# A two-layer backbone with a product-key mixer: layer 1's modulation moved into layer 0's one-hot blocks, and the advance steps regrouped

## The chip, the cores and the metric

The kernel runs on one core of a Trainium2 chip. The metric is the time of one execution on the device in microseconds (us), the median over runs. The names of the engines are those of the profile: PE is TensorE (matmuls), PEld its weight loads, DVE is VectorE, ACT is ScalarE, POOL is GpSimd, SP is the queue from which nearly all transfers are issued.

## The reference

256 latent tokens and 256 context tokens, width 1024, go through two layers. Every layer first turns the conditioning vectors into six rows of modulation, normalizes and modulates, mixes the tokens (attention and retention in layer 0, differential attention in layer 1), and then sends each token to 128 of 16384 experts:

```
mod = jax.nn.silu(c) @ ada_w[l] + ada_b[l]          # (1024,) @ (1024, 6144), and the same for c_ctx
sh1, sc1, g1, sh2, sc2, g2 = jnp.split(mod, 6)
x = x + g1 * mixer(modulate(rmsnorm(x), sh1, sc1))
h2 = modulate(rmsnorm(x), sh2, sc2)
# _peer, for each block of 128 tokens
s = einsum('thpd,hpnd->thpn', (h2 @ w_q).reshape(128, 8, 2, 128), keys)
s_top, i_top = lax.top_k(s, 16)                     # for each of 8 heads and 2 halves
cand = s_top[:, :, 0, :, None] + s_top[:, :, 1, None, :]
best, pos = lax.top_k(cand, 16)                     # 16 of 256 sums; eid is the pair of indices
gate = softmax(best)
act = gelu(einsum('td,thkd->thk', h2, u_tab[eid]))
f = einsum('thk,thkd->td', gate * act, v_tab[eid])
x = x + g2 * f
```

## The kernel before

Everything is fp32, the large products as sums of split parts (high and low) on PE. The stages follow one another: the even mixer (layer 0), layer 0's routing, its one-hot blocks, its main loop over 128 groups of 128 experts, then the odd mixer (layer 1) and the same three stages of the mixer of experts for layer 1.

**Modulation.** `mod_group` computes one of six groups of a layer's modulation in eight k-slices. A slice is one load of 512 KB of `ada_w` (tile `w`, by `wload`) and eight small matmuls into `mod_ps` (four column quarters, two parts each). After the eighth slice the rows go through `mrow` and two matmuls into `mcol`. Before the change, four groups of layer 0 and two of layer 1 are spread as fill over the even mixer; the other four groups of layer 1 are spread over the odd mixer, where DVE makes the products (`macc`) and PE only sums over the partitions at the end of a group.

**Routing.** `peer_route` makes the queries and scores head by head on PE, copies them (ACT, `S`), and `top16` on DVE takes the 16 best of each half. `route_heads` is called twice for each stream of 256 tokens (two streams in layer 0, one in layer 1), with r=0 in the middle and with r=1 behind the last scores: candidate sums `cand`, a second `top16`, and the indices by one-hot comparisons (`ab`, `abf`, `rk`, `oh`). The results, transposed (`trp`), are the slots `sl` of the blocks.

**u steps.** `First` runs ahead of the main loop: `ahead` yields one step for each group of 128 experts, 27 of them in layer 0 and 22 in layer 1. A step loads `ur` (512 KB), splits it into `uh` (ACT) and `ul` (GpSimd or DVE), and makes 24 matmuls into `u_ps`; ACT then takes the gelu. Steps are issued during `route_heads` with r=1, then between the blocks, then behind them.

**One-hot blocks.** 24 in layer 0, 12 in layer 1. `find` and `weigh` are four large operations of DVE, `join` is 32 matmuls into `g_ps` and `keep` copies to `stage` (ACT) and writes 1 MB to `gd`. `pipeline` issues the blocks in a staggered way, so that different blocks stand in different stages. Afterwards `G` is read back from `gd`, and the first product `y` of the main loop needs it.

What order the work has is decided by the order in which the code issues it: each engine and the SP queue take their instructions in order.

Of the kernel before, what the change touches and what calls it, by code (L numbers as in the profile page):

```python
# [19 lines left out]
D = 1024  # L20
# [10 lines left out]
FILL0, FILL1 = (1, 2, 2, 1), (0, 2, 2, 2)  # L31
NUS = (2, 3)
NRAW, NWQ = 3, 6
# [5 lines left out]
ROUTE, AFTER = (12, 9), (3, 4)  # L39
# [3 lines left out]
def backbone(ctx: ExitStack, tc: tile.TileContext, x, cx, ccT, ada_w, ada_b, ada_rows, n1g, n2g, ev_in, ev_out,  # L43
# [114 lines left out]
    def wload(src, kn, nn):  # L158
        w = P["wp"].tile([128, kn, nn], F32, tag="w", name="w", bufs=NW)
        last["w"] = nc.sync.dma_start(w, src.rearrange("(k p) n -> p k n", p=128))  # L160
        return w
# [42 lines left out]
    def mod_group(d, l, g, both=True):  # L204

# [8 lines left out]
        if both:  # L214
            p = mm([128, 256], "mod_ps")
        else:
            acc = P["z"].tile([128, D], F32, tag="macc", name="macc", bufs=1)
        for k in range(KD):
            w = wload(ada_w[l, k * 128:(k + 1) * 128, g * D:(g + 1) * D], 1, D)
            if both:  # L220
                matmuls(silu_c[:, k, :], w[:, 0], k == 0, k == KD - 1)
            elif k == 0:
                nc.vector.tensor_scalar(acc, w[:, 0], silu_c[:, 0, 0:1], None, op0=OP.mult)
            else:
                nc.vector.scalar_tensor_tensor(acc, w[:, 0], silu_c[:, k, 0:1], acc, op0=OP.mult, op1=OP.add)
            yield
        if not both:
            p = mm([128, 256], "mod_ps")
            matmuls(ones[:, 0:32], acc, True, True)
# [376 lines left out]
    def odd_mixer(mod, fill):  # L606
# [27 lines left out]
        with in_order():  # L634
            norm_T((0,), aff1, hi, lo, t2)
            project(hi, lo, od_in, 0, 512, 512, tiles[:2], to_tiles(qq, 512), fill, FILL1[0])
        norm_T((1,), aff1, hi, lo, t2)
        project(hi, lo, od_in, 512, 1024, 512, tiles[:2], to_tiles({tk: qq[tk][:, 512:] for tk in qq}, 512), fill, FILL1[0])
        for tk in (0, 1):
            heads_T(qT, tk, qq[tk])  # L640
        project(hi, lo, od_in, 1024, 2048, 512, tiles, to_tiles(kk, 512), fill, FILL1[1])
# [4 lines left out]
        def values_of(n):  # L646
            project(hi, lo, od_in, 2048 + n * 512, 2560 + n * 512, 512, tiles, to_tiles({tk: vv[tk][:, n * 512:] for tk in vv}, 512), fill, FILL1[2 + n])
            if n:
                for _ in fill:
                    pass  # L650
# [73 lines left out]
    def route_heads(r, m, ix, ixb, i12, gate, step):  # L724
# [5 lines left out]
        for a in range(2):  # L730
            nc.scalar.copy(ixb[:, a].rearrange("p n (i h) -> p i h n", i=2), ix[:, :, hs, a, :])
        cand = wk([128, 2, 4, 112], "cand")
        for i in range(2):
            nc.gpsimd.tensor_tensor(cand[:, i, :, 0:64].rearrange("p h (a b) -> p h a b", a=4),
                                    m[:, i, hs, 0, 0:4, None].to_broadcast([128, 4, 4, 16]),
                                    m[:, i, hs, 1, None, :].to_broadcast([128, 4, 4, 16]), op=OP.add)
            nc.gpsimd.tensor_tensor(cand[:, i, :, 64:112].rearrange("p h (a b) -> p h a b", a=12),
# [4 lines left out]
        for i in range(2):  # L742
            for h in range(4):
                top16(best[:, i, h, :], pos[:, i, h, :], cand[:, i, h, :])
                if h % 2:
                    step()
        pi = pos.rearrange("p i h k -> p k (i h)").bitcast(I32)
# [6 lines left out]
        nc.scalar.copy(abf, ab.rearrange("p a f k n -> p a f (k n)"))  # L754
# [7 lines left out]
        nc.vector.tensor_add(rf, rf, abf[:, :, 0, :])  # L762
        for a in range(2):
# [9 lines left out]
            step()  # L773
        g = wk([128, 8, 16], "gate_e")
        b3 = best.rearrange("p i h k -> p (i h) k")
        nc.vector.tensor_sub(g, b3, b3[:, :, 0:1].to_broadcast([128, 8, 16]))
        nc.scalar.activation(g, g, AF.Exp)
        gs = sm([128, 8], "gs")
        nc.vector.tensor_reduce(gs, g, axis=AX.X, op=OP.add)
        nc.vector.reciprocal(gs, gs)  # L780
        nc.gpsimd.tensor_mul(gate[:, :, r * 64:(r + 1) * 64].rearrange("p i (h k) -> p i h k", h=4), g.rearrange("p (i h) k -> p i h k", i=2),
# [489 lines left out]
```

## Time and profile before

| | us |
|---|---|
| median of 3 runs | 2745.76 (2743.51 to 2748.35) |
| the profiled execution, its own time | 2754.86 |
| its span, first to last instruction | 2752.8 |
| PE busy | 2570.1 (93%) |
| DVE busy | 2055.0 (75%) |
| ACT busy | 1120.4 (41%) |
| POOL busy | 1043.0 (38%) |

Rough borders of the stages in the profiled execution: even mixer to 333 us, layer 0's routing to 546, its blocks and the rest of the u steps to 717, its main loop to 1690, odd mixer to 1930, layer 1's routing to 2054, its blocks and u steps to 2150, its main loop to 2740. A row of a timeline gives the start, the duration, the engine, the line of the kernel, the operation with output and inputs, and in brackets how long the engine stood idle before it and whose end released it.

### The profile page before, as it was taken

The numbers are of one execution on the slowest core, as the hardware profiler recorded it, in microseconds if no ns is written. First come the engines' busy times: TensorE is split into PE (matmuls) and PEld (weight loads), VectorE is DVE, ScalarE is ACT, GpSimd is POOL, SyncE is SP. The second block draws the span as 40 slices with busy tenths as digits, with TensorE's granted clock in tenths as the row PEclk, the third lists the DMA queues.
The fourth block names the chain that finished last, engine by engine and source line by source line (L and its number), as shares of the span: only waits on it lengthen the run. The fifth ranks groups of instructions, "written<-read, shape, count | busy, mean of one in ns | idle before, by whom it ended". The sixth has DMA issues, their size and how long they took to land.

```text
span 2752.8 us, 39475 instructions
## 1 busy us (share of the span) xinstructions
PE 2570.1 (93%) x14787; PEld 2237.7 (81%) x14787; DVE 2055.0 (75%) x3753; ACT 1120.4 (41%) x1832; POOL 1043.0 (38%) x643
## 2 busy tenths in 40 slices
PE   7899996899999999999999998989859999999997
PEld 4776775899989888899898876756859899999995
DVE  3535579898677776677677776787888788888888
ACT  3234432444333333333333334234535455555543
POOL 0201042300477677667766610100520344434431
PEclk9999997899999999999999998999979999999999
DMA  8562431255888888888888875632537999999996
GB/s 285 178 207 96 138 99 33 85 207 221 293 288 287 288 287 297 286 294 298 296 308 279 289 251 165 226 129 89 179 108 257 341 347 345 348 349 332 355 326 217
DMA packets 263552, 667.80 MB, mean 243 GB/s; under 512 B 21760, under 2 KB 108544, under 8 KB 258752
## 3 DMA queue, kind: packets, MB, share of 16 engines
q1 hardware_dynamic: 204176, 458.81, 48.9%
q0 software_dynamic: 55296, 201.35, 20.2%
q10 hardware_dynamic: 3888, 5.11, 0.6%
q8 instruction: 116, 1.90, 0.3%
q14 instruction: 76, 0.62, 0.1%
HBM read 621.88 MB, written 42.47 MB: 241 GB/s over the span
## 4 chain that ended last, share of the span: by engine, by line
PE 70%; DVE 13%; issue 5%; POOL 5%; DMA 4%; ACT 1%; ACTq 0%; POOLq 0%; SPq 0%; DVEq 0%
PE y L1038 24%; PE u_ps L911 9%; PE u_ps L910 9%; PE u_ps L909 9%; PE g_ps L985 4%; PE z_ps L318 2%; PE z_ps L319 2%; PE z_ps L320 2%; POOL ul L155 2%; POOL row L859 2%; DMA w<-in_ada_w_dram 1%; PE trp L170 1%; PE q_ps L806 1%; PE q_ps L807 1%; PE q_ps L805 1%
## 5 line engine op out<-in xcount | busy, mean ns | idle before, releaser
L909 PE MATMUL u_ps<-hi,uh 128*128 128x384 f32 (+1 forms) x2048 | 635.7, 310 | 42.8 <-ACT uh L154 35.6
L1038 PE MATMUL y<-vh,ww 128*128 128x512 f32 x2304 | 661.4, 397 | 7.0 <-ACT ww L1019 6.1
L911 PE MATMUL u_ps<-hi,ul 128*128 128x384 f32 (+1 forms) x2048 | 637.5, 311 | 24.8 <-POOL ul L155 13.9
L910 PE MATMUL u_ps<-lo,uh 128*128 128x384 f32 (+1 forms) x2048 | 634.6, 310 | 0.0
L1038 PEld LDWEIGHTS y<-vh,ww 128*128 128x128 f32 x2304 | 425.0, 189 | 95.0 <-ACT ww L1019 11.4
L859 POOL DMA_INDIRECT row<-in_u_tab_dram,eid x192 | 291.4, 1518 | 424.4 <-DVE w L1015 152.0
L909 PEld LDWEIGHTS u_ps<-hi,uh 128*128 128x128 f32 x2048 | 396.0, 193 | 53.7 <-ACT uh L154 36.9
L911 PEld LDWEIGHTS u_ps<-hi,ul 128*128 128x128 f32 x2048 | 395.2, 193 | 32.5 <-POOL ul L155 20.4
L154 ACT CAST vh<-vr 128x1024 fp32r<-128x1024 f32 x256 | 267.7, 1046 | 368.4 <-PE y L1038 339.1
L1038 PE MATMUL y<-vl,ww 128*128 128x512 f32 x1280 | 402.7, 395 | 0.1
L910 PEld LDWEIGHTS u_ps<-lo,uh 128*128 128x128 f32 x2048 | 395.6, 193 | 8.7
L155 POOL TENSOR_TENSOR ul<-ur,uh 128x1024 fp32r<-128x1024 f32 x116 | 311.0, 2682 | 240.0 <-ACT uh L154 238.7
L865 DVE SCALAR_TENSOR_TENSOR row<-row,h 128x1024 f32<-128x1024 f32 x192 | 299.7, 1577 | 112.6 <-DMA row<-in_u_tab_dram,eid 112.3
L859 POOL DMA_INDIRECT row<-in_v_tab_dram,eid x192 | 288.9, 1505 | 245.0 <-DVE w L1015 142.0
L155 DVE TENSOR_TENSOR vl<-vr,vh 128x1024 fp32r<-128x1024 f32 x256 | 312.4, 1220 | 73.3 <-ACT vh L154 73.0
L871 DVE SCALAR_TENSOR_TENSOR f<-row,coef,f 128x1024 f32<-128x1024 f32 x190 | 289.9, 1526 | 100.2 <-DMA row<-in_v_tab_dram,eid 98.7
L1038 PEld LDWEIGHTS y<-vl,ww 128*128 128x128 f32 x1280 | 240.4, 188 | 59.3 <-DVE vl L155 3.9
L154 ACT CAST uh<-ur 128x1024 fp32r<-128x1024 f32 x256 | 268.3, 1048 | 20.3 <-DMA ur<-in_u_t_dram 10.9
L1019 ACT CAST ww<-w 128x384 fp32r<-128x384 f32 (+1 forms) x256 | 110.7, 432 | 330.5 <-DVE w L1015 211.6
L155 DVE TENSOR_TENSOR ul<-ur,uh 128x1024 fp32r<-128x1024 f32 x140 | 171.4, 1224 | 83.9 <-ACT uh L154 83.7
L916 ACT ACTIVATE act<-u_ps 128x384 f32<-128x384 f32 (+1 forms) x256 | 105.1, 410 | 284.8 <-PE u_ps L911 284.7
L151 POOL TENSOR_TENSOR rs<-rs,nhalf 128x4 f32<-128x4 f32 (+2 forms) x19 | 22.4, 1177 | 461.4 <-DVE rs L150 347.6
(270 smaller groups left out, 3755.9 us busy)
## 6 DMA issues: line engine op xcount, KB each, us to landing
ur<-in_u_t_dram SPq DMA_DIRECT2D x256, 512.0 KB, 5.6
vr<-in_v_tab_dram SPq DMA_DIRECT2D x256, 512.0 KB, 6.1
w<-in_ada_w_dram SPq DMA_DIRECT2D x96, 512.0 KB, 4.7
gd<-stage SPq DMA_DIRECT2D x36, 1024.0 KB, 4.8
G<-gd SPq DMA_DIRECT2D x16, 1536.0 KB, 11.9
w<-in_w_q_dram SPq DMA_DIRECT2D x64, 256.0 KB, 3.4
w<-in_od_in_dram SPq DMA_DIRECT2D x24, 512.0 KB, 5.4
G<-gd SPq DMA_DIRECT2D x16, 768.0 KB, 8.6
```

The source lines that it names most:

```text
L154: nc.scalar.copy(hi, src)
L155: (eng or nc.vector).tensor_tensor(lo, src, hi.bitcast(F32), op=OP.subtract)
L859: nc.gpsimd.indirect_dma_start(out=r[n], out_offset=None, in_=v_tab if n >= S else u_tab, in_offset=bass.IndirectOffsetOnAxis(ap=eid[:, n ...
L865: nc.vector.scalar_tensor_tensor(t, t, 1.0, h2, op0=OP.mult, op1=OP.mult, accum_out=coef[:, n:n + 1])
L871: nc.vector.scalar_tensor_tensor(f, t, coef[:, j:j + 1], f, op0=OP.mult, op1=OP.add)
L909: nc.tensor.matmul(p, uh[:, k, :], hi[:, k, 0:n], start=k == 0, stop=False)
L910: nc.tensor.matmul(p, uh[:, k, :], lo[:, k, 0:n], start=False, stop=False)
L911: nc.tensor.matmul(p, ul[:, k, :], hi[:, k, 0:n], start=False, stop=k == KD - 1)
L916: nc.scalar.activation(a, self.ps.pop(e), AF.Gelu)
L985: nc.tensor.matmul(v["p"][t // 4][:, t % 4, :], o2[:, t // 4, :, t % 4], o1[:, t // 4, :, t % 4], start=n == 0, stop=n == 1)
L1019: nc.scalar.copy(ww[:, 0:ntok], w)
L1038: nc.tensor.matmul(y[j][:, d, :], x1, x2[:, d * 512:(d + 1) * 512], start=e == 0 and n == 0, stop=e == 127 and n == len(sums) - 1)
```

## The change

All six groups of layer 1's modulation are computed on PE in the one-hot blocks of layer 0, two k-slices ahead of each block, from a pool of two buffers for `w`. The even and the odd mixer have no layer 1 modulation left. The u steps are dealt out anew: in layer 0 six directly behind the last scores, 12 in `route_heads` with r=1, five between the blocks, four behind them (before: 12 in the routing, 12 between the blocks, 3 behind); in layer 1 five, nine, four and four (before: nine, nine and four). All `ul` of the routing are on GpSimd, `uh` and `ul` are made at different places, and in the matmuls of a step all `uh` stand before all `ul`. In `route_heads` with r=1 the candidate sums and the cast `abf` go to DVE, and the copies `ixb`, the exponential and the gate are moved.

```
-FILL0, FILL1 = (1, 2, 2, 1), (0, 2, 2, 2)
+FILL0 = (1, 2, 1, 1)
+NRAW, NWQ, NMOD = 3, 6, 2
-ROUTE, AFTER = (12, 9), (3, 4)
+STEPS = (6, 12, 4), (5, 9, 4)
...
     def mod_group(d, l, g):
+        p = mm([128, 256], "mod_ps")
         for k in range(KD):
             w = wload(ada_w[l, k * 128:(k + 1) * 128, g * D:(g + 1) * D], 1, D)
+            matmuls(silu_c[:, k, :], w[:, 0], k == 0, k == KD - 1)
             yield
...
+        eng = nc.vector if r else nc.gpsimd
         for i in range(2):
-            nc.gpsimd.tensor_tensor(cand[:, i, :, 0:64].rearrange("p h (a b) -> p h a b", a=4),
+            eng.tensor_tensor(cand[:, i, :, 0:64].rearrange("p h (a b) -> p h a b", a=4),
...
-        nc.scalar.copy(abf, ab.rearrange("p a f k n -> p a f (k n)"))
+        (nc.vector.tensor_copy if r else nc.scalar.copy)(abf, ab.rearrange("p a f k n -> p a f (k n)"))
...
-                S = wk([128, 2, 2, 128], "S", bufs=3)
+                S = wk([128, 2, 2, 128], "S", bufs=8)
...
         tail.clear()
+        first.step(STEPS[l][0])
-            first.eng = nc.gpsimd if i % 7 < 5 else nc.vector
-            for _ in range(ROUTE[l] * i // total, ROUTE[l] * (i + 1) // total):
+            for _ in range(STEPS[l][1] * i // total, STEPS[l][1] * (i + 1) // total):
                 next(first.steps)
...
+        def high(self, e):
+                nc.scalar.copy(h, self.ur[e])
+        def low(self, e, eng=nc.gpsimd):
+                eng.tensor_tensor(t, self.ur.pop(e), self.us[e][0].bitcast(F32), op=OP.subtract)
...
             for e in range(self.R):
                 self.load(e + 2)
+                self.low(e, self.eng)
                 self.gelu(e - 1)
+                self.high(e + 1)
                 self.mm(e)
-                self.split(e + 1, self.eng)
                 yield
...
+                left = R - sum(STEPS[l])
+                def between(i):
+                    first.step(left * (i + 1) // n - left * i // n)
+                    with in_order():
+                        for _ in range(2):
+                            next(fill, None)
+                with pools(wp=1, mods=1), banks(1, 1):
+                    last["nw"] = NMOD
+                    pipeline(blocks, {i: lambda i=i: between(i) for i in range(n)}, False)
+                first.step(STEPS[l][2])
...
-        even_mixer(mod, mods(*[(mod, 0, g) for g in (2, 3, 4, 5)], (mod1, 1, 0), (mod1, 1, 1)))
+        even_mixer(mod, mods(*[(mod, 0, g) for g in (2, 3, 4, 5)]))
-        odd_mixer(mod1, mods(*[(mod1, 1, g, False) for g in (2, 3, 4, 5)]))
+        odd_mixer(mod1)
```

On the SP queue, at the start of layer 0's blocks, this stood before: the writes `gd` of the blocks with loads `ur` of the u steps between them.

```order
L896 DMA ur<-in_u_t_dram 128x1024 x11
L991 DMA gd_4794<-stage 128x2048
L896 DMA ur<-in_u_t_dram 128x1024
L991 DMA gd_4794<-stage 128x2048 x2
L896 DMA ur<-in_u_t_dram 128x1024
```

Now the same place reads as follows; `w` are the 512 KB slices of modulation.

```order
L881 DMA ur<-in_u_t_dram 128x1024 x15
L160 DMA w<-in_ada_w_dram 128x1024 x8
L986 DMA gd_4876<-stage 128x2048
L160 DMA w<-in_ada_w_dram 128x1024 x2
L986 DMA gd_4876<-stage 128x2048
L881 DMA ur<-in_u_t_dram 128x1024
L160 DMA w<-in_ada_w_dram 128x1024 x2
L986 DMA gd_4876<-stage 128x2048
L160 DMA w<-in_ada_w_dram 128x1024 x2
```

Four pairs of slices are asked for ahead of the first `gd`, and each later pair stands directly behind the write of a block. As the pool has two buffers, each pair also waits for the matmuls of the pair before it.

On PE, between the first and the second block of layer 0, this is how it stands now (a row `x8` of `mod_ps` is one pair of slices).

```order
L980 MATMUL g_ps<-ol,o_4910 128x128
L210 MATMUL mod_ps<-w,silu_c 32x256 x8
L980 LDWEIGHTS o_4929
L980 MATMUL g_ps<-oh,o_4929 128x128
```

Before, the second block's matmuls followed directly there. Three pairs stand ahead of the first block, and one ahead of each of the next 21; u steps stand in front of four of these.

On ACT, behind the last scores of layer 0, the indices of stream 0 were copied (`ixb`) ahead of the first casts `uh` of this stretch.

```order
L818 COPY S<-k_ps 128x512 x3
L731 CAST ixb_2942<-ix_2941 128x8x16 x2
L154 CAST uh<-ur 128x1024
L916 ACT_TABLE_LOAD
L916 ACTIVATE act<-u_ps 128x384
L154 CAST uh<-ur 128x1024
```

Now 11 casts `uh` stand between the last `S` and that copy; the end of them reads so.

```order
L909 ACTIVATE act<-u_ps 128x384
L886 CAST uh<-ur 128x1024
L732 CAST ixb_2828<-ix_2827 128x8x16 x2
L736 ACT_TABLE_LOAD
L736 ACTIVATE gate_e<-gate_e 128x128
L909 ACT_TABLE_LOAD
```

The casts have moved ahead of the copy, and the exponential of the gate has moved up from behind the one-hot comparisons.

## Rows read from the trace of the kernel before

**Rows 1.** The page: shares of the chain that ended last.

```profile
PE 70%; DVE 13%; issue 5%; POOL 5%; DMA 4%; ACT 1%; ACTq 0%; POOLq 0%; SPq 0%; DVEq 0%
```

**Rows 2.** Windows: stretch, length, busy us of each engine, granted clock, DMA share, GB/s.

```profile
core 0: us, PE busy (x) PEld busy (x) DVE busy (x) ACT busy (x) POOL busy (x), PEclk, DMA share, GB/s
177.00:290.00 113.00, 113.00 (x714) 77.95 (x714) 47.87 (x125) 49.63 (x123) 12.49 (x13) 1.00 0.30 99
484.00:546.00 62.00, 54.47 (x276) 53.24 (x277) 54.30 (x192) 22.64 (x37) 20.73 (x13) 0.89 0.31 94
546.00:717.00 171.00, 163.06 (x1151) 157.70 (x1150) 135.21 (x118) 80.52 (x133) 3.49 (x3) 0.93 0.61 225
2054.00:2150.00 96.00, 83.77 (x694) 82.16 (x693) 72.27 (x65) 45.86 (x78) 6.40 (x6) 0.89 0.72 263
```

**Rows 3.** Timeline of PE in the even mixer: a slice of modulation and what follows.

```profile
196.96 0.64 PE L211 MATMUL mod_ps<-w,silu_c 128*32 128x256 f32 x8
197.53 1.09 PE L512 MATMUL o_ps<-pT,zv 128*64 128x128 f32 x8
```

**Rows 4.** Timeline of PE: waits behind layer 0's scores and in layer 1's u steps.

```profile
481.34 0.69 PE L909 MATMUL u_ps<-hi,uh 128*128 128x384 f32 x1 [17.41 <-ACT uh L154]
...
2138.65 0.53 PE L909 MATMUL u_ps<-hi,uh 128*128 128x192 f32 x1 [7.11 <-ACT act L916]
```

**Rows 5.** Timeline of DVE: one-hot comparisons in both routings, first block of layer 0.

```profile
546.19 1.22 DVE L972 TENSOR_TENSOR o<-iota,sl 128x2048 f16<-128x2048 f16 x1
...
1986.91 2.04 DVE L765 TENSOR_TENSOR oh<-rk,ranks 128x2048 bf16<-128x2048 bf16 x1
...
1994.58 1.20 DVE L765 TENSOR_TENSOR oh<-rk,ranks 128x2048 bf16<-128x2048 bf16 x1
...
2034.79 1.97 DVE L755 TENSOR_SCALAR abf<-abf 128x128 bf16<-128x128 bf16 x1 [3.93 <-ACT abf L754]
```

**Rows 6.** Timeline of POOL in the same stretch of layer 1.

```profile
1985.21 7.11 POOL L155 TENSOR_TENSOR wl<-w,wh 128x512 fp32r<-128x512 f32 x4 [0.80 <-ACT wh L154]
```

**Rows 7.** Timeline of PE in the blocks, and in the u steps behind them.

```profile
557.12 0.30 PE L985 MATMUL g_ps<-ol,o 128*128 128x128 f16 x1
...
560.44 0.30 PE L985 MATMUL g_ps<-ol,o 128*128 128x128 f16 x1
...
691.35 0.42 PE L909 MATMUL u_ps<-hi,uh 128*128 128x384 f32 x1
...
712.49 0.34 PE L909 MATMUL u_ps<-hi,uh 128*128 128x384 f32 x1
...
716.72 0.62 PE L1038 MATMUL y<-vh,ww 128*128 128x512 f32 x2
...
2123.08 0.34 PE L909 MATMUL u_ps<-hi,uh 128*128 128x192 f32 x1
...
2125.83 0.27 PE L909 MATMUL u_ps<-hi,uh 128*128 128x192 f32 x1
```

**Rows 8.** Timeline of the SP queue behind the last block of layer 0.

```profile
692.26 0.32 SPq L991 DMA_DIRECT2D gd<-stage  x1
692.67 3.27 SPq L896 DMA_DIRECT2D ur<-in_u_t_dram  x3
```

**Rows 9.** DMA issues from 546 to 692 us: KB each, median us to landing.

```profile
gd<-stage SPq DMA_DIRECT2D x23, 1024.0 KB, 4.8
ur<-in_u_t_dram SPq DMA_DIRECT2D x10, 512.0 KB, 5.6
```

**Rows 10.** The tensor `ada_w`: all 96 loads of slices.

```profile
DMA to landing us min/median/max: 3.4/4.7/13.0
```

**Rows 11.** Timeline of PE: a slice between waits for loads, a block behind a wait.

```profile
8.07 1.08 PE L211 MATMUL mod_ps<-w,silu_c 128*32 128x256 f32 x8 [0.31 <-DMA w<-in_ada_w_dram]
...
586.53 0.28 PE L985 MATMUL g_ps<-ol,o 128*128 128x128 f16 x1 [0.97 <-DVE ol L978]
```

**Rows 12.** Window behind that wait.

```profile
586.50:590.00 3.50, 3.47 (x30) 3.47 (x30) 3.47 (x3) 2.40 (x4) 0.00 (x0) 0.52 0.95 309
```

**Rows 13.** The page: GB/s moved, in 40 equal slices of the span.

```profile
GB/s 285 178 207 96 138 99 33 85 207 221 293 288 287 288 287 297 286 294 298 296 308 279 289 251 165 226 129 89 179 108 257 341 347 345 348 349 332 355 326 217
```

More of the change, by code (lines that the diff above doesn't have):

```diff
@@ L746, in route_heads @@
                     step()
+        for a in range(2):
+            nc.scalar.copy(ixb[:, a].rearrange("p n (i h) -> p i h n", i=2), ix[:, :, hs, a, :])
+        g = wk([128, 8, 16], "gate_e")
+        b3 = best.rearrange("p i h k -> p (i h) k")
+        nc.vector.tensor_sub(g, b3, b3[:, :, 0:1].to_broadcast([128, 8, 16]))
+        nc.scalar.activation(g, g, AF.Exp)
         pi = pos.rearrange("p i h k -> p k (i h)").bitcast(I32)
@@ L910, in mm @@
                     nc.tensor.matmul(p, uh[:, k, :], lo[:, k, 0:n], start=False, stop=False)
+                for k in range(KD):
                     nc.tensor.matmul(p, ul[:, k, :], hi[:, k, 0:n], start=False, stop=k == KD - 1)
@@ L920, in ahead @@
                 self.load(e)
-            self.split(0)
+            self.high(0)
             yield
@@ L924, in ahead, with step, dense_experts @@
                 self.load(e + 2)
+                self.low(e, self.eng)
                 self.gelu(e - 1)
+                self.high(e + 1)
                 self.mm(e)
-                self.split(e + 1, self.eng)
                 yield
-        def step(self):
+        def step(self, n=1):
             with in_order():
-                next(self.steps, None)
-    def dense_experts(l, slots, hi, lo, tiles, g2, upools, first, rows, half=False):
+                for _ in range(n):
+                    next(self.steps, None)
+    def dense_experts(l, slots, hi, lo, tiles, g2, upools, first, rows, half=False, fill=iter(())):
         nt = len(slots)
@@ L995, in dense_experts @@
                 blocks = [tuple(block(j, c)) for j in range(nt) for c in range(8) if j * 8 + c < ntc]
-                n = len(blocks) + 4
-                left, first.eng = R - ROUTE[l] - AFTER[l], nc.vector
-                pipeline(blocks, {i: lambda i=i: [first.step() for _ in range(left * i // n, left * (i + 1) // n)] for i in range(n)},
-                         False)
-                for _ in first.steps:
-                    pass
+                n, first.eng = len(blocks) + 4, nc.vector
+                left = R - sum(STEPS[l])
[6 more added lines that the diff above has]
+                    last["nw"] = NMOD
+                    P["small"], small = P["mods"], P["small"]
+                    pipeline(blocks, {i: lambda i=i: between(i) for i in range(n)}, False)
+                    for _ in fill:
+                        pass
+                    P["small"] = small
+                    last.pop("nw")
+                first.step(STEPS[l][2])
             ring = st.enter_context(pool_(name="ring", bufs=2))
@@ L1051, in dense_experts @@
             load_G(0)
+            first.low(R)
             weigh(0)
@@ L1067, in dense_experts @@
                     weigh(e + 1)
-                    first.split(e + R + 1, nc.vector if half else nc.gpsimd)
+                    first.high(e + R + 1)
+                    first.low(e + R + 1, nc.vector if half else nc.gpsimd)
                     next(side, None)
```

63 lines of the change are left out of this document (21 added, 42 removed).

## The prediction, made before the changed kernel was run

> **What bounds the kernel now.** I read the chain that ended last first: PE holds 70% of it, DVE 13%, DMA 4% [rows 1]. So a change counts where PE's work is shortened, or where PE waits. The windows then show the four stretches that the change touches [rows 2]. In the even mixer (177 to 290 us) PE is busy for all of 113 us: a matmul less is time less. In layer 0's routing (484 to 546) PE and DVE are busy 54.5 and 54.3 of 62 us; DVE's chain decides when the blocks begin, and ahead of it PE stood still for 17.41 us, because its first u step waited for a cast of ACT [rows 4]. In layer 0's blocks (546 to 717) PE is busy 163 of 171 us and DVE 135: PE is the bound, with DMA at 0.61. In layer 1's blocks (2054 to 2150) PE has 84 of 96 us. Both main loops keep their instructions, and I price them at nothing.
>
> **The sum, part by part,** against the profiled execution's 2754.9 us; the median of the runs is 2745.8, 0.3% less, and I carry the sum over to the median.
>
> (a) *Even mixer.* Two groups of layer 1, 16 slices, leave it. A slice takes 0.57 us of PE from its start to that of the next instruction [rows 3], in a stretch without a gap: 16 x 0.57 = **-9.1 us**. The loads were no wait there (DMA share 0.30).
>
> (b) *Layer 0's routing, up to the first `find` at 546.19* [rows 5]. DVE loses some 7 us: the `ul` operations of this stretch, and waits for `cand` and `abf`, less the candidate sums that it takes over. But all 18 `ul` are now on GpSimd, up to 12 of them beside DVE's one-hot comparisons. Such a comparison took 2.04 us while GpSimd worked (1985 to 1992) and 1.20 after it [rows 5, 6]; four loops, each with about three times 0.84 us of such work, give up to 10 us. `ixb` and the exponential now stand behind 11 casts on ACT, which go at the pace of PE's u steps; I allow 1.4 us for that. Bounds: -5 if little overlaps, +9 if nearly all does. -7 + 10 + 1.4 is **+4**, which I take: six more steps keep GpSimd busy in just this stretch.
>
> The GPSIMD Engine Reference of the Trainium skill (section 1, Specifications) says that GpSimd shares its SBUF interfaces with VectorE, with contention for instructions that have two SBUF inputs. The 2.04 against 1.20 us agree; the rule speaks against moving every `ul` there, and for taking `cand` away, and by it the sum would not differ from that by the rows.
>
> (c) *Layer 0, from the first `find` to the first `y`: 170.5 us* (546.19 to 716.72 [rows 5, 7]). PE's own work hardly changes. A block of `g_ps` is 32 x (560.44 - 557.12)/28 = 3.8 us, a u step 716.72 - 712.49 = 4.23 [rows 7]. Before: 24 x 3.8 + 12 x 4.23 = 142; after: 24 x 3.8 + 5 x 4.23 + 48 x 0.57 = 140. What is new is a wait. The pool has two slices. Count from the end of a block's matmuls. Its `gd` is issued 0.9 us later (691.35 to 692.26) and a load behind it 0.4 after that [rows 7, 8]. `gd` lands 4.8 after issue, a `ur` issued right behind it 5.6 after its own, so 6.0 after `gd`'s [rows 9]: half a MB more costs 1.2. Two slices behind `gd` have then landed 4.8 + 1.2 + 1.2 = 7.2 after it, 8.1 after the block. PE wants the second slice after this round's pair (1.14), the next block (3.8) and the first slice (0.57), at 5.5. If every round stands still for s, PE wants the slice 2s later, once for this round's pair and once for the next, while `gd` still leaves on time: 2s + 5.5 = 8.1, s = 1.3 us. Of the 21 rounds with a pair and a block four have a u step in front that covers it: 17 x 1.3 = 22. Ahead of the first block three pairs pass through two buffers, two loads of 4.7 [rows 10] one after the other, so that block starts some 8.7 us after the first `find` rather than 3.7; of this 3.4 is in PE's sum already, +1.6. Behind the blocks six u steps take 25.4 at full pace, as long as the five of before took with gaps (691.35 to 716.72); 0 to +2, say +1. PE's sum -2; so -2 + 22 + 1.6 + 1 = **+22.6**. Lower bound 0: no load late (3.4 us is the shortest [rows 10]). Upper bound +40: with these waits PE falls to the lower clock more often. The gap of 0.97 at 586.53 was followed by a granted clock of 0.52, about the lower level of 1.2 GHz [rows 11, 12], and a slice between waits took 1.08 where it else takes 0.64 [rows 3, 11]; 48 x 0.44 = 21 more, of which I take none, because the 21 rounds wait on loads and a slower slice eats partly into that wait.
>
> The page DMA: Bandwidth & Descriptors of the Trainium skill (Anatomy of one DMA) gives a transfer 2.0 us and its bytes at 436 GB/s, which for 2 MB is an estimate of 6.8 us in place of 7.2. No run here shows a transfer by itself; by that figure s would be 1.1 and this part 3 us cheaper.
>
> (d) *Odd mixer.* Four groups' closing matmuls, one slice's worth each, 4 x 0.57 = 2.3, and DVE's products, which were mostly beside PE: **-3** (0 to -8).
>
> (e) *Layer 1.* The cast `abf` on DVE removes its wait of 3.93 us [rows 5]. Five u steps run in the routing's idle time, so the blocks hold 4 instead of 9. A u step there is 2.75 us of PE (2123.08 to 2125.83 [rows 7]): 12 x 3.8 + 9 x 2.75 = 70 before, 57 after; DVE, 12 x 4 x 1.22 plus 9 `ul` of 1.22 (70) before, 63 after, is then the bound: -7. The wait of 7.11 for `act` [rows 4] stays. **-11** (-5 to -14).
>
> Sum: -9.1 + 4 + 22.6 - 3 - 11 = **+3.5 us**, 0.13%: on the scale of the median **2749 us**.
>
> **Rivals.**
> *R1, the loads are not late (faster).* If the two slices land within 5.5 us of the block's end, s is 0 and the 22 go: 2749 - 22 = **2727**. For it: 24 MB in 546 to 717 is a mean of 225 GB/s [rows 2], and the main loop of layer 1 holds 341 to 355 GB/s [rows 13]. Against: with 24 MB more, 62 MB in 170 us would be 365 GB/s, above all these slices, and the pair needs `gd` out of the way in just those rounds. It decides at a landing of 6.3 us after `gd`'s issue for all 2 MB, against my 7.2.
> *R2, the lower clock (slower).* The waits leave PE at 1.2 GHz, and each slice costs up to 0.44 us more: 2749 + 10 to 21, **2765**. For it: three quarters of the rounds would hold a wait of the size that was seen ahead of the drop at 586.53. Against: the block behind it did not lengthen, 30 matmuls in 3.47 us [rows 12], 0.116 each as elsewhere.
> *R3, the routing gives it all away (slower).* `ixb` stands behind 11 casts, so a slow u step delays DVE's comparisons, and GpSimd slows them: (b) +9 and the 11 us of (e) halved: 2749 + 5 + 5.5, **2760**. Against: PE's 11 steps at 4.23 us end about when DVE's last `top16` does.
>
> **How the numbers follow.** My forecast, loads late by about 1.3 us a round, with parts (b), (d) and (e) within their bounds: 0.45, 2741 to 2759. R1 0.25, R2 0.18, R3 0.12. The range from **2724 to 2768** takes in R1 and R2 with the bounds of (b) and (e) cut at 2 in 10. A change within 0.2% (5.5 us) is about what a measurement of this kernel can't tell from none. Faster by more: R1 and 0.07 of the forecast's 0.45, **0.31**; within: 0.27 of the forecast and 0.03 of R3, **0.30**; slower: **0.39**.
>
> **What would show it.** In the profile after, PE in the even mixer would be 9 us shorter. In layer 0's routing the 17.41 us in front of the first u step would be gone, while the first `find` comes 4 us later than before counted from the end of the even mixer; comparisons of about 2 us beside GpSimd's `ul`. In layer 0's blocks PE would wait some 1.3 us for `w` in 17 rounds, with granted clocks below 1 behind the waits. In layer 1 the blocks would begin 4 us earlier and be 7 us shorter. The forecast is wrong if the `w` loads land with PE still in the block (R1), if slices take 1.08 us throughout (R2), or if the main loops change, for which I see no reason.

## The result, and the profile after

The changed kernel takes **2789.62 us** (median of 4 runs, 2785.61 to 2796.82) against 2745.73 before: ratio **1.0162**, 95% interval 1.0144 to 1.0179. It is 44 us slower; 2749 was forecast, and 2768 was the upper end of the range.

The profiled execution of after spans 2784.4 us, 31.6 more than that of before (2752.8). The other 12 us lie in the executions: the profiled one of before was 9.1 us above its median, that of after (2786.49) 3.1 below. This table is worked out from the timelines: each stretch ends where the named first or last instruction starts or ends.

| stretch | before | after | change | forecast |
|---|---|---|---|---|
| (a) to the first query matmul of layer 0 | 333.9 | 322.6 | -11.3 | -9.1 |
| (b) from there to the first `find` (540.51) | 212.3 | 217.9 | +5.6 | +4 |
| (c) to the last block's matmuls | 145.4 | 187.8 | **+42.4** | |
| (c) to the first `y` | 25.1 | 25.4 | +0.3 | +22.6 for both |
| layer 0's main loop | 979.9 | 963.0 | **-16.9** | 0 |
| (d) to layer 1's last score | 300.4 | 298.6 | -1.7 | -3 |
| (e) to the first `find` of layer 1 | 56.6 | 60.4 | **+3.8** | -4 |
| (e) to the first `y` of layer 1 | 98.0 | 106.1 | **+8.0** | -7 |
| the rest | 601.2 | 602.6 | +1.4 | 0 |

The same code takes different times in different traces. Layer 0's main loop took 963.0 to 973.0 us in the 14 traces of kernels with the new order of a u step, and the stretch (a) 331 to 338 us in the seven with the old modulation. A difference of a few us between two traces is therefore not yet an effect.

The windows of after, first over layer 0's blocks (from the first `find` to the last `g_ps`), which answer to the third of [rows 2], then a part of layer 0's main loop:

```profile
core 0: us, PE busy (x) PEld busy (x) DVE busy (x) ACT busy (x) POOL busy (x), PEclk, DMA share, GB/s
540.50:728.30 187.80, 149.06 (x1257) 114.85 (x1258) 121.72 (x116) 64.75 (x108) 0.00 (x0) 0.80 0.76 272
...
900.00:1100.00 200.00, 200.00 (x1002) 181.45 (x1001) 152.66 (x187) 70.38 (x96) 145.89 (x81) 1.00 0.89 297
```

In the blocks PE stands idle for 38.7 of 187.8 us, at a mean granted clock of 0.80. In this part of the main loop it has no idle time at all. What PE waits for in the blocks is in the view of the tile `mod_ps` (us, times). PE and its weight loads are counted together there, so each wait counts twice; PE alone is in the view of `in_ada_w_dram`, in the second fence:

```profile
  DMA w<-in_ada_w_dram: 75.1, 60
```

```profile
  PE mod_ps L210: 34.9, 30
```

PE's timeline of after shows the waits: two ahead of the first block, the longest one, and a pair of rounds in the regular rhythm.

```profile
545.54 1.08 PE L210 MATMUL mod_ps<-w,silu_c 128*32 128x256 f32 x8 [2.96 <-DMA w<-in_ada_w_dram]
...
550.41 1.08 PE L210 MATMUL mod_ps<-w,silu_c 128*32 128x256 f32 x8 [1.81 <-DMA w<-in_ada_w_dram]
...
633.49 1.08 PE L210 MATMUL mod_ps<-w,silu_c 128*32 128x256 f32 x8 [8.04 <-DMA w<-in_ada_w_dram]
...
647.67 0.64 PE L210 MATMUL mod_ps<-w,silu_c 128*32 128x256 f32 x8 [1.13 <-DMA w<-in_ada_w_dram]
649.21 0.64 PE L210 MATMUL mod_ps<-w,silu_c 128*32 128x256 f32 x8 [0.91 <-DMA w<-in_ada_w_dram]
654.13 0.64 PE L210 MATMUL mod_ps<-w,silu_c 128*32 128x256 f32 x8 [0.41 <-DMA w<-in_ada_w_dram]
655.37 0.64 PE L210 MATMUL mod_ps<-w,silu_c 128*32 128x256 f32 x8 [0.60 <-DMA w<-in_ada_w_dram]
```

From one round's first slice to the next (647.67 to 654.13) it is 6.46 us; without waiting it would be a pair and a block, 1.14 + 3.8 = 4.9. Not every round is like that: of the 34.9 us, 6.8 lie ahead of the first block and 8.6 in the round of the long wait; the other 16 rounds with a pair and no u step in front waited 0 to 3.4 us, 1.2 on average. The SP queue at the two places, first at the long wait, then at the regular rhythm:

```profile
628.20 0.33 SPq L224 DMA_DIRECT2D gate<-mrow  x1
628.63 0.88 SPq L160 DMA_DIRECT2D w<-in_ada_w_dram  x2
...
647.19 0.33 SPq L986 DMA_DIRECT2D gd<-stage  x1
648.37 1.87 SPq L160 DMA_DIRECT2D w<-in_ada_w_dram  x2
```

The two loads of a round go out 1.2 us and more behind the write `gd`, when the matmuls of the round before have freed their buffers, and the second has landed by 655.37, 8.2 us after `gd` was issued. At 628 the queue had first to wait for `mrow` (VectorE finished it at 628.2), because the write of the gate stands ahead of the loads.

### The profile page after: what moved, and what is told of

Its sections match the earlier page's. It is cut to its first block, busy times and chain, and to the rows that moved or that the text cites. A ratio compares the mean times of both kernels' runs of the same rounds, so it can differ in the third digit from the quotient of the medians.

```text
span 2784.4 us, 39857 instructions
## 1 busy us (share of the span) xinstructions
PE 2582.1 (93%) x15011; PEld 2238.3 (80%) x15011; DVE 2045.2 (73%) x3718; ACT 1121.5 (40%) x1829; POOL 1074.9 (39%) x649
## 3 DMA queue, kind: packets, MB, share of 16 engines
q1 hardware_dynamic: 204176, 458.81, 48.9%
## 5 line engine op out<-in xcount | busy, mean ns | idle before, releaser
L901 PE MATMUL u_ps<-hi,uh 128*128 128x384 f32 (+1 forms) x2048 | 587.9, 308 | 16.2 <-ACT uh L886 16.2
L902 PE MATMUL u_ps<-lo,uh 128*128 128x384 f32 (+1 forms) x2048 | 588.4, 309 | 0.0
L844 POOL DMA_INDIRECT row<-in_u_tab_dram,eid x192 | 300.3, 1564 | 478.0 <-ACT act L909 199.2
L892 POOL TENSOR_TENSOR ul<-ur,uh 128x1024 fp32r<-128x1024 f32 x134 | 342.6, 2558 | 278.4 <-ACT uh L886 275.5
L850 DVE SCALAR_TENSOR_TENSOR row<-row,h 128x1024 f32<-128x1024 f32 x192 | 305.6, 1612 | 74.2 <-DMA row<-in_u_tab_dram,eid 72.7
L904 PE MATMUL u_ps<-hi,ul 128*128 128x384 f32 (+1 forms) x2048 | 341.8, 310 | 12.3 <-DVE ul L892 9.8
L856 DVE SCALAR_TENSOR_TENSOR f<-row,coef,f 128x1024 f32<-128x1024 f32 x190 | 302.1, 1590 | 53.2 <-DMA row<-in_v_tab_dram,eid 50.8
L904 PEld LDWEIGHTS u_ps<-hi,ul 128*128 128x128 f32 x2048 | 310.6, 193 | 14.5 <-DVE ul L892 11.6
L1045 PEld LDWEIGHTS y<-vl,ww 128*128 128x128 f32 x1280 | 240.4, 188 | 60.3 <-DVE vl L155 3.6
L892 DVE TENSOR_TENSOR ul<-ur,uh 128x1024 fp32r<-128x1024 f32 x122 | 149.4, 1225 | 74.0 <-ACT uh L886 72.6
```

The source lines that it names most:

```text
L844: nc.gpsimd.indirect_dma_start(out=r[n], out_offset=None, in_=v_tab if n >= S else u_tab, in_offset=bass.IndirectOffsetOnAxis(ap=eid[:, n ...
L850: nc.vector.scalar_tensor_tensor(t, t, 1.0, h2, op0=OP.mult, op1=OP.mult, accum_out=coef[:, n:n + 1])
L856: nc.vector.scalar_tensor_tensor(f, t, coef[:, j:j + 1], f, op0=OP.mult, op1=OP.add)
L892: eng.tensor_tensor(t, self.ur.pop(e), self.us[e][0].bitcast(F32), op=OP.subtract)
L901: nc.tensor.matmul(p, uh[:, k, :], hi[:, k, 0:n], start=k == 0, stop=False)
L902: nc.tensor.matmul(p, uh[:, k, :], lo[:, k, 0:n], start=False, stop=False)
```

## The experiments

Each was timed beside the kernel before on the same chip; ratios, with their 95% intervals, are to that. Each experiment names the kernel that it starts from.

### What the modulation in the blocks costs

**Modulation put back** into the changed kernel: the old `mod_group`, the fill of the even and the odd mixer, and nothing between the blocks.

```
-                with pools(wp=1, mods=1), banks(1, 1):
-                    pipeline(blocks, {i: lambda i=i: between(i) for i in range(n)}, False)
+                pipeline(blocks, {i: lambda i=i: between(i) for i in range(n)}, False)
-        even_mixer(mod, mods(*[(mod, 0, g) for g in (2, 3, 4, 5)]))
+        even_mixer(mod, mods(*[(mod, 0, g) for g in (2, 3, 4, 5)], (mod1, 1, 0), (mod1, 1, 1)))
-        odd_mixer(mod1)
+        odd_mixer(mod1, mods(*[(mod1, 1, g, False) for g in (2, 3, 4, 5)]))
```

> The changed kernel with layer 1's modulation put back where it was (two groups in the even mixer on PE, four in the odd mixer on VectorE); all else of the change stays. Theory 1 (the loads of the modulation in layer 0's blocks are the loss): the 42 us that the blocks gained go, the 11 us of the even mixer come back, 2790 - 42 + 11 = 2759 us, and PE waits for no w between 540 and 730 us. Rival (the regrouped u steps and the routing are the loss): stays at 2775 to 2790.

Measured: 2751.47 us, ratio 1.0026 (1.0009 to 1.0042). Of the 44 us, 38 go with the modulation, 7 more than I expected. In its trace the blocks, from the first `find` to the last `g_ps`, are 52 us shorter than in after, and 9 shorter than in the kernel before:

```profile
547.40:683.30 135.90, 114.61 (x865) 108.52 (x866) 119.04 (x102) 63.20 (x104) 0.00 (x0) 0.78 0.49 194
```

That gain of the regrouped steps is lost elsewhere: what stays of the change is by itself no gain, 0.3% on the slow side.

**Only the modulation moved**, from the kernel before: the same lines the other way, with the old u steps.

> The kernel before with only layer 1's modulation moved into layer 0's blocks. Theory 1: the even mixer 11 us shorter, the blocks longer by 20 (where the 12 u steps that still stand among them cover loads) to 42: 2755 to 2777 us. Rival (the move is harmless by itself): 2735 to 2746.

Measured: 2798.61, ratio 1.0180 (1.0148 to 1.0211): slower than either theory said. My figure of 20 to 42 left something out. In the kernel before PE has no room in the blocks: 12 u steps still stand there, and the 48 slices, 48 x 0.57 = 27 us, come on top of the waits. From the first `find` to the last `g_ps` it took 205.2 us (145.4 before), 175.3 of them busy. The u steps that the change moves out of the blocks are thus what makes room for the modulation.

**All matmuls, but only two loads:**

```
+        if "nw" in last:
+            held = last.setdefault("held", [])
+            if len(held) == last["nw"]:
+                held.append(held.pop(0))
+                return held[-1]
         w = P["wp"].tile([128, kn, nn], F32, tag="w", name="w", bufs=last.get("nw", NW))
+        if "nw" in last:
+            held.append(w)
```

> The changed kernel in which the blocks load only the first two slices of the modulation and use them for all 48, so that all matmuls stay and 46 loads of 512 KB are left out (layer 1's modulation is then of other weights). Theory 1 (PE waits for the loads, and the lower clock follows from these waits): the blocks come back to about the 145 us of before, 2790 - 40 = 2750 us, clock near 0.93 in them. Rival (the added matmuls and pool borders themselves, or the lower clock by itself): 2775 or more.

Measured: 2745.95, ratio 1.0006 (0.9990 to 1.0021): the whole loss is gone. The window of its blocks, to be read beside that of after:

```profile
541.10:687.40 146.30, 138.84 (x1257) 115.63 (x1258) 121.38 (x116) 64.27 (x108) 0.00 (x0) 0.95 0.47 184
```

The same 1257 matmuls take 146.3 us instead of 187.8. PE's idle time falls from 38.7 to 7.5 us, so 31 us were waiting; its busy time falls from 149.1 to 138.8 with the clock at 0.95 instead of 0.80, so the other 10 are matmuls at a lower clock behind the waits. The extra matmuls alone make the blocks 10 us longer (146.3 against 135.9 with the modulation put back), and the shorter mixers give that back: the whole kernel takes 2745.95 us against 2751.47. The loads are shown to be the cause of the loss.

**Three buffers for `w`** in place of two:

```
-NRAW, NWQ, NMOD = 3, 6, 2
+NRAW, NWQ, NMOD = 3, 6, 3
```

> The changed kernel with three buffers for w in the blocks instead of two. If a round waits because a load can only be issued when the matmuls of the pair before it have freed a buffer, the first load of a pair goes out 0.8 us and the second about 1.5 us earlier, in some 20 rounds: 15 to 25 us less, 2765 to 2775 us. Rival (the 1 MB write gd ahead of the loads sets their landing, whatever the buffers): 2782 to 2792.

Measured: 2782.17, ratio 1.0143 (1.0118 to 1.0169): 7 us less than the changed kernel, with intervals that overlap, and not 15 to 25. The first load of a pair now leaves right behind `gd`, 0.4 us after it and not 1.2, as its SP queue shows:

```profile
633.03 0.33 SPq L986 DMA_DIRECT2D gd<-stage  x1
633.46 2.71 SPq L160 DMA_DIRECT2D w<-in_ada_w_dram  x2
```

PE's waits for `w` are 29.9 us, where after has 34.9. So the buffers were one limit, and another lay right behind it.

**The gate's transfers on GpSimd's queue:**

```
-            nc.sync.dma_start(d[g], rows)
+            (nc.gpsimd if "nw" in last else nc.sync).dma_start(d[g], rows)
```

(and the same for `brow`).

> The changed kernel with the two small transfers of a modulation group that ends in a gate (brow, gate) issued by GpSimd in the blocks, where it is idle, instead of SP. If the one wait of 8.04 us for w at 633.49 comes from the write of the gate standing ahead of the loads on SP, waiting for mrow, then 6 us go: 2783 us, and no wait above 3 us. Rival (the wait has another cause, and it stays): 2790.

Measured: 2783.20, ratio 1.0136 (1.0118 to 1.0155), 6.4 us less, as expected, though here too the intervals overlap and so do not show it. What the trace shows by itself: PE's wait at that place fell to 2.83, and is now for `mrow` itself:

```profile
631.30 1.08 PE L210 MATMUL mod_ps<-w,silu_c 128*32 128x256 f32 x8 [2.83 <-DVE mrow L222]
```

### What the regrouped steps do

**Only the order within a u step changed**, in the kernel before:

```
                     nc.tensor.matmul(p, uh[:, k, :], lo[:, k, 0:n], start=False, stop=False)
+                for k in range(KD):
                     nc.tensor.matmul(p, ul[:, k, :], hi[:, k, 0:n], start=False, stop=k == KD - 1)
```

> The kernel before with only the order of a u step's matmuls changed: all of uh first, then all of ul. If this order is what made layer 0's main loop 17 us shorter, PE's waits for ul go there: 2729 to 2738 us. Rival (the 17 us are the chance of one profiled execution, or come from the casts' new places): 2743 to 2748.

Measured: 2735.94, ratio 0.9964 (0.9950 to 0.9978): faster by 10 us. And **the kernel before once more**:

> The kernel before once more, for a second profiled execution. If its layer 0 main loop took 980 us only in the first profiled execution, because of PE's chance waits for ul of GpSimd, it takes 965 to 972 here and the span is 2740 to 2745; if the order of a step's matmuls costs 16 us in every execution, it takes 978 to 982 again.

Its main loop took 973.0 us, between the two figures expected; its span was 2745.2. The windows of 900 to 1100 us, of the kernel before and of the one with `ul` last:

```profile
900.00:1100.00 200.00, 193.85 (x951) 172.93 (x950) 142.01 (x180) 66.61 (x91) 137.94 (x77) 0.99 0.84 288
```

```profile
900.00:1100.00 200.00, 200.00 (x1000) 181.09 (x999) 154.33 (x187) 68.42 (x94) 147.53 (x81) 1.00 0.89 299
```

PE had waits for GpSimd's `ul` of up to 2.75 us before, at places that differ between executions (the second one had its longest in this loop, 1.47 us, at 961.94). With 16 matmuls of `uh` ahead, `ul` has time, and the loop takes 963.4 us. The times show that this edit gains some 10 us in the kernel before. That they are the main loop's waits for `ul` is what this pair of traces says, but single traces do not settle it: the run above with only the modulation moved has the old order, and its loop took 966.0 us, while among the kernels with the new order it took up to 973.0, in some of them with waits for `uh` and `ul` of 2 to 5 us in all. So of the 17 us in the table about 10 fit this edit, and 7 are within what traces of the kernel before differ by.

**`ul` made one step ahead again**, in the kernel with the modulation put back:

```
             self.high(0)
+            self.low(0, self.eng)
             yield
             for e in range(self.R):
                 self.load(e + 2)
-                self.low(e, self.eng)
                 self.gelu(e - 1)
                 self.high(e + 1)
                 self.mm(e)
+                self.low(e + 1, self.eng)
                 yield
```

> The changed kernel with the modulation put back (as in the first experiment, 2751.5 us) and ul made one step ahead of its matmuls again. If layer 1's blocks are longer because the ul of a step is asked for in that same step, PE's three waits of 2.3 to 2.6 us for VectorE's ul and the 0.77 ones of layer 0 go: 6 to 10 us less, 2742 to 2746. Rival (VectorE's work sets the blocks, and a wait only moves): 2749 to 2752.

Measured: 2739.69, ratio 0.9971 (0.9956 to 0.9986), 12 us less than without, more than I expected. What it removed is this wait, three times in layer 1's blocks of after (and in layer 0's 0.77 us three times):

```profile
2088.90 1.14 PE L904 MATMUL u_ps<-hi,ul 128*128 128x192 f32 x8 [2.62 <-DVE ul L892]
```

From layer 1's first block to the last it is 62.4 us now, against 69.4 with the modulation put back and 70.7 in after. In the change `low(e)` and `mm(e)` stand in one step; PE, in order, waits for a VectorE that is busy with blocks, and the blocks behind wait for PE. In layer 0 the stretch from the first `find` to the last `g_ps` is shorter by as much, 129.4 us against 135.9.

**No early u step in layer 1**, on top of that:

```
-STEPS = (6, 12, 4), (5, 9, 4)
+STEPS = (6, 12, 4), (0, 9, 4)
```

> The kernel of the ul-ahead experiment (2739.7 us), with no u step of layer 1 directly behind its last scores: 0 instead of 5, so nine stand between its blocks. If GpSimd's ul slow VectorE in layer 1's routing, fewer of them overlap it and the first find comes 2 to 4 us earlier, while the blocks take some 3 us more: 2737 to 2741. Rival (the five early steps are a gain that the blocks need): 2745 to 2750.

Measured: 2727.62, ratio 0.9932 (0.9911 to 0.9952), 12 us less, where I expected 3 at most: from layer 1's last score to its first `find` it is 48.9 us instead of 60.3 (56.6 before), 11.4 less where I expected 2 to 4. The reason stands in after's timelines, of VectorE and of GpSimd, between the end of `top16` and the one-hot comparisons:

```profile
2050.33 2.46 DVE L741 TENSOR_SCALAR ab<-pos 128x128 int32<-128x128 int32 x1
...
2053.01 2.51 DVE L744 CAST abf<-ab 128x512 bf16<-128x512 int32 x1
...
2055.55 2.38 DVE L745 TENSOR_SCALAR abf<-abf 128x128 bf16<-128x128 bf16 x1
...
2058.29 2.42 DVE L751 TENSOR_TENSOR rk<-rk,far 128x256 bf16<-128x256 bf16 x1
```

```profile
2050.13 5.10 POOL L892 TENSOR_TENSOR ul<-ur,uh 128x1024 fp32r<-128x1024 f32 x2 [0.23 <-ACT uh L886]
2055.49 2.39 POOL L892 TENSOR_TENSOR ul<-ur,uh 128x1024 fp32r<-128x1024 f32 x1 [0.26 <-ACT uh L886]
2058.17 2.39 POOL L892 TENSOR_TENSOR ul<-ur,uh 128x1024 fp32r<-128x1024 f32 x1 [0.29 <-ACT uh L886]
```

Four operations of VectorE that else take 0.2 to 0.5 us each last as long as one `ul` of GpSimd, 2.4 us, one for each of four `ul`; the short ones between them keep their 0.2 to 0.3. That is 8.5 of the 11.4 us. The other 2.9 are a wait for ACT's exponential, which is gone without the early steps too:

```profile
2063.87 0.29 DVE L754 TENSOR_REDUCE gs<-gate_e 128x8 f32<-128x128 f32 x1 [2.84 <-ACT gate_e L736]
```

Without the five early steps the last `ul` ends while `top16` still runs, and the same operations have VectorE to themselves (its `TENSOR_SCALAR` and the end of `top16`, then GpSimd):

```profile
2012.87 0.27 DVE L722 FIND_INDEX8 pos<-best,cand 128x8 uint32<-128x112 f32 x1
...
2013.24 0.26 DVE L754 TENSOR_SCALAR ab<-pos 128x128 int32<-128x128 int32 x1
```

```profile
2010.62 2.37 POOL L907 TENSOR_TENSOR ul<-ur,uh 128x1024 fp32r<-128x1024 f32 x1 [0.29 <-ACT uh L901]
2016.28 1.21 POOL L771 TENSOR_TENSOR gate<-gate_e,gs 128x128 f32<-128x128 f32 x1 [3.28 <-DVE gs L770]
```

`top16` itself isn't hurt: `FIND_INDEX8` and its kin take 0.26 to 0.28 beside an `ul` as without one.

**Layer 1's routing as before**, layer 0's regrouped: a switch in `route_heads` and `peer_route` that restores, for layer 1, the old places of `ixb`, `cand`, `abf`, gate and steps.

```
+        if old:
+            indices()
-        eng = nc.vector if r else nc.gpsimd
+        eng = nc.vector if r and not old else nc.gpsimd
...
+            if old:
+                step()
+        if old:
+            gates(exps())
```

> The kernel of the ul-ahead experiment with layer 1's routing as in the kernel before (steps 0, 9, 9, 4, ul of the one-hot comparisons on VectorE, cand on GpSimd, abf on ScalarE); layer 0 stays regrouped. If the regrouping gains in layer 0 and loses in layer 1's routing, as the two traces say (from the last score to the first y 158 us against 150 with the kernel before and ul last): 2739.7 - 8 = 2732 us. Rival (the difference is chance of the executions): 2738 to 2742.

Measured: 2733.97, ratio 0.9954 (0.9937 to 0.9970), as expected to 2 us. The old routing is 54.3 us from score to `find`, so the new one is a gain of some 5 (48.9) if GpSimd's `ul` stay clear of VectorE's short operations. That gain is not that of `cand` and `abf`, which cost VectorE 2.2 us there: in its rows the old routing has three `ul` of its own, 3.7 us, and two short operations that last 4.5 us longer beside GpSimd's `ul`. The edit moves all of this at once, so no part is shown by itself.

### Why the loads are late

**Two groups, one slice per block**: 16 slices taken from the even mixer, with the change's pool of two buffers, and `next(fill)` once between blocks instead of twice.

```
-        even_mixer(mod, mods(*[(mod, 0, g) for g in (2, 3, 4, 5)], (mod1, 1, 0), (mod1, 1, 1)))
+        even_mixer(mod, mods(*[(mod, 0, g) for g in (2, 3, 4, 5)]))
...
+                        for _ in range(1):
+                            next(fill, None)
```

> As the run with layer 1's old routing, and two groups of layer 1's modulation (16 slices) moved from the even mixer into layer 0's blocks, one slice per block rather than two. A slice is then asked for a whole block earlier than it is wanted and half as many bytes pass, so PE does not wait, and the blocks are bound by VectorE: the even mixer's 9 to 11 us are gained, 2721 to 2723 us. Rival (any load among the blocks makes PE wait): 2732 or more.

Measured: 2739.98, ratio 0.9970 (0.9956 to 0.9985): no gain, 6 us worse than without (the intervals overlap). My expectation fell. **The same with two per block:**

> The same 16 slices, two per block: the same bytes and matmuls, in the first eight rounds. If the pair's rhythm is what makes PE wait, three pairs ahead of the first block cost 5 to 9 us and five rounds 1.5 each: 12 to 17 us more than with one per block, 2733 to 2740. Rival (only the number of bytes counts): as with one per block.

Measured: 2741.57, ratio 0.9972 (0.9954 to 0.9990), the same, which is what the rival said. From the first `find` to the last `g_ps` it took 144.4 and 148.2 us, against 131.1 with no slice there. With one per block about every second slice waited, 7 of 16:

```profile
583.04 0.64 PE L211 MATMUL mod_ps<-w,silu_c 128*32 128x256 f32 x8 [2.33 <-DMA w<-in_ada_w_dram]
```

and this is its SP queue:

```profile
576.93 0.33 SPq L1026 DMA_DIRECT2D gd<-stage  x1
577.36 0.37 SPq L160 DMA_DIRECT2D w<-in_ada_w_dram  x1
581.38 0.33 SPq L1026 DMA_DIRECT2D gd<-stage  x1
581.80 0.37 SPq L160 DMA_DIRECT2D w<-in_ada_w_dram  x1
```

A buffer had been free for a block, yet each load leaves 0.4 us after a `gd`, because it stands behind it in the queue, and `gd` leaves only when ACT has copied the block. The load of 577.36 has landed at 583.04, 5.7 us later, as long as a `ur` behind `gd` took [rows 9]. What stood open then was order or bytes. **Each load issued two slices ahead in the code**, one slice per block, on the fastest kernel so far (2727.62):

```
+    def top_up():
+        todo = last.get("todo")
+        while todo and len(last["ready"]) < last["nw"]:
+            l, g, k = todo.pop(0)
+            last["ready"].append(wload(ada_w[l, k * 128:(k + 1) * 128, g * D:(g + 1) * D], 1, D))
...
-            w = wload(ada_w[l, k * 128:(k + 1) * 128, g * D:(g + 1) * D], 1, D)
+            w = last["ready"].pop(0) if "nw" in last else wload(ada_w[l, k * 128:(k + 1) * 128, g * D:(g + 1) * D], 1, D)
             matmuls(silu_c[:, k, :], w[:, 0], k == 0, k == KD - 1)
+            if "nw" in last:
+                top_up()
             yield
```

> The fastest kernel so far (2727.6 us: ul one step ahead, no early u step in layer 1, modulation as in the kernel before) with 16 slices moved from the even mixer into layer 0's blocks, one per block, and each load issued two slices ahead of its use, so that on SP it stands in front of the write gd that it stood behind. If the order on SP made PE wait: no wait for w behind the first three slices, the even mixer's 9 to 11 us gained, 2717 to 2721 us. Rival (bytes beside gd make it wait): waits of 2 us stay in every other round, 2728 to 2735.

Measured: **2721.39**, ratio **0.9916** (0.9894 to 0.9938), the fastest median here. One wait for `w` is left, ahead of the first block. Its SP queue, and its view of `mod_ps` (33.4 us, 16 times, in the run with one slice per block and no loads ahead; both count PE and its weight loads):

```profile
572.71 0.33 SPq L160 DMA_DIRECT2D w<-in_ada_w_dram  x1
573.08 0.43 SPq L1010 DMA_DIRECT2D gd<-stage  x1
577.16 0.33 SPq L160 DMA_DIRECT2D w<-in_ada_w_dram  x1
577.53 0.47 SPq L1010 DMA_DIRECT2D gd<-stage  x1
```

```profile
  DMA w<-in_ada_w_dram: 7.2, 2
```

The same bytes, but each load now stands 0.4 us ahead of `gd`, and it leaves 8.4 us ahead of its use (that of 572.71 is wanted at 581.13) where it had 5.7. So the bytes were not the cause, and the place of the load in the order of the code was. Whether it helps by standing in front of the write or by being early is not told apart, since here one brings the other. The stretch takes 132.4 us, 3 more than without the slices (129.2), and (a) is 11.4 shorter, though the trace that it is compared with has the longest (a) of all with the old modulation. By the medians the gain over the kernel without the slices is 6 us; the intervals overlap (0.9911 to 0.9952 there), so the times alone do not show it.

**Loads ahead, two slices per block:**

> The same with two slices per block. Order theory: each load goes out when the matmuls that free its buffer end, about when gd does, so waits of about 1 us stay in the eight rounds and two loads pass ahead of the first block: 2724 to 2732 us. Rival (bytes alone): as with one per block.

Measured: 2736.18, ratio 0.9965 (0.9951 to 0.9979), 4 us above what I expected; 146.2 us for the stretch. Here the buffers bind again: with two buffers and two slices a round, a load cannot leave before the round's own matmuls. **Loads ahead, all 48 slices, three buffers**, on the changed kernel:

> The changed kernel with three buffers for w and each load issued three slices ahead of its use. Order theory: loads leave ahead of gd and most of PE's waits go, down to what 2 MB per round need at the 340 to 385 GB/s that the trace holds elsewhere (5.5 to 6.2 us against 4.9, so 10 to 25 us stay of 42): 2758 to 2772 us. Rival (buffers and bytes were all of it): as with three buffers alone, 2780.

Measured: 2763.52, ratio 1.0065 (1.0043 to 1.0087): 26 us less than the changed kernel, 19 less than three buffers alone, as the order theory said. Against three buffers alone only the place of the loads in the code differs, so this is the cleanest of these comparisons. 18 us stay. Its blocks:

```profile
536.30:705.30 169.00, 144.39 (x1257) 114.69 (x1258) 121.88 (x116) 59.78 (x108) 0.00 (x0) 0.87 0.85 303
```

PE is idle for 24.6 of 169 us, at 303 GB/s. Of this 5.74 us are one wait at the place of the gate, for which the profile names no releaser, and 14.4 are waits for `w`. How much of the remainder is bytes was not told apart.

## Why the prediction was wrong, point by point

Three steps failed: the sign of (e), where two waits were left out; the size of (c), where the lower clock was taken at nothing, the gate's write left out and the start sized too small; and the price of nothing for layer 0's main loop.

(a) and (b) were right: -11.3 for -9.1, +5.6 for +4. In (b) the mechanism was that of the sum: in VectorE's rows of layer 0's routing the one-hot products and sums took 10.2 us more, for +10 in the sum; stream 0's one-hot sums took 5.55 us beside two `ul` of GpSimd, those of stream 1, with GpSimd idle, 1.47.

```profile
497.53 5.55 DVE L764 TENSOR_TENSOR oh<-oh 128x1024 bf16<-128x1024 bf16 x3
...
531.80 1.47 DVE L764 TENSOR_TENSOR oh<-oh 128x1024 bf16<-128x1024 bf16 x3
```

```profile
496.38 6.09 POOL L892 TENSOR_TENSOR ul<-ur,uh 128x1024 fp32r<-128x1024 f32 x2
```

(c) had the right mechanism and half the size: +42.7 for +22.6, just beyond the upper bound of 40. Three things were sized too small, shown by the trace and by the runs named. The start: from the first `find` to the first block it is 13.1 us and not 8.7, since slices there also run at half pace (1.08 us in the rows at 545 and 550). The gate's write on SP, which I had not priced though it stands in the queue: about 5 us (the wait of 8.04 against 2.83 with the gate on GpSimd's queue). And the lower clock, of which I took none: 10 us of PE's busy time (the run with two loads), of which the start has a part. The wait of a round, 1.3 in the sum, was 1.2 on average in the 16 other rounds; as it ranged from 0 to 3.4, and the sum had one rhythm for all, that the mean came out is partly luck. The sum for a round also missed the order: I counted the load from the freed buffer and from `gd` at once, and the run with one slice per block shows that a load behind `gd` is late even where a buffer is free.

The Trainium skill's page DMA: Bandwidth & Descriptors (Anatomy of one DMA) gives 2.0 us and the bytes at 436 GB/s for a transfer issued by GpSimd; the prediction applied that to transfers of SP, for an estimate of 6.8 us from the issue of `gd`. The trace has 8.2 for the 2 MB, with the loads leaving 1.2 to 2.7 us behind it. So of the two figures the estimate by the page, which made the wait smaller, was further off than the 7.2 by the rows.

R1 (loads not late) fell with PE's 34.9 us of waits for `w`. Two of its readings were wrong: 225 GB/s in 546 to 717 are 38 MB and not 24 (the sum behind it has the right 62), and layer 1's main loop holds 326 to 355 GB/s and not 341 to 355 [rows 13]. R2 was a part: the lower clock is 10 of the 42 us, not the cause. Of R3, that GpSimd slows VectorE held for layer 1.

(e) failed in sign: +11.8 for -11. I counted `ul` operations and took them as moved into idle time. Two waits took the place of what went. In the routing, GpSimd's `ul`, paced by five more steps, reached into VectorE's short operations and ACT's exponential came late (together +3.8; without the early steps -7.7 against before). I had priced this meeting in layer 0 and left it out in layer 1. In the blocks, `ul` now stood in the same step as its matmuls (+5.7 from the first block to the last, gone with `ul` ahead). The diff shows it, and I had read it as a mere regrouping. Behind the blocks another 3.4 us came: PE waits twice for `uh` there, 3.73 and 6.05 us, where it had waited once, 7.11. Without the early steps there is one wait again; why was not tested.

The main loop, priced at nothing, became 17 us shorter; about 10 of them fit the order of `ul` and `uh`, as far as the times of that edit in the kernel before carry over. The rows for it were there to be read in the trace of before: 6 us of PE idle in the window of 200 us shown above. Two errors thus partly hid each other; without this one the change would have been some 10 us slower still.

(d): -1.7 for -3. VectorE's products in the odd mixer were all but free, so taking them away gave little back.

## What to carry to other kernels

A load that is issued next to its use stands, in an in-order queue, behind whatever that place in the code waits for; before counting buffers or bytes, read in the order of the queue what each load stands behind, and issue it early enough in the code. Where work moves onto an engine "beside" another, look at which operations of the other it will meet: here long elementwise work on GpSimd was free beside `top16` and cost VectorE 2 us at each of four short operations behind it. And an operand that is needed last in a chain of matmuls should be made last and multiplied last: one line moved gave 10 us in the kernel before.

## What the runs showed of the hardware that was not expected

VectorE's short operations did not just slow down beside GpSimd's `ul`, they lasted to about its end (2057.93 against 2057.88 us, 2060.71 against 2060.56): 0.2 to 0.5 us became 2.4, four times, also for operations with one input (`TENSOR_SCALAR`, `CAST`), while `MAX8` and `FIND_INDEX8` kept their 0.27. The Trainium skill's GPSIMD Engine Reference (section 1, Specifications) names VectorE instructions in a two-port mode or with two SBUF inputs as those that contend for the shared interface. That fits the row with two inputs (`rk`, 2.42 us against 0.29); whether the one-input operations ran in such a mode, no row shows.

Where PE's waits were many and short, the granted clock stayed low on average (0.80 in the blocks of after, 0.78 in those of the kernel at 2727.62 us), which cost 10 us in the first, where PE is the bound, and nothing that shows in the second, where VectorE is.
